# FFN of a hybrid attention/mLSTM step: weights requested a column block sooner, squares of gate and up summed by one product early in the block, group scale two units later

## The chip, the cores and the metric

The kernel runs on one core of a Trainium2 chip. The metric is device time in microseconds (us) of one execution; three executions were timed, and one more was taken with a profile. TensorE (PE, with its weight loads PEld), VectorE (DVE), ScalarE (ACT) and GpSimd (POOL) compute; SyncE (SP) issues most of the transfers.

## The reference, cut to what matters

One layer is computed for 128 context tokens and 1024 latent tokens (1152 rows, model width 1024): attention and a matrix-memory head group side by side, merged by an output projection, then a SwiGLU FFN of inner width 2816. The change touches the FFN alone:

```python
def swiglu(h, w_gu, w_down):
    g, u = jnp.split(h @ w_gu, 2, axis=-1)
    return (jax.nn.silu(g) * u) @ w_down
...
    h2 = rmsnorm(x, norm2_w) * (1 + sc2) + sh2
    x = x + g2 * swiglu(h2, w_gu, w_down)
```

`w_gu` is 1024 x 5632 (gate, then up), `w_down` 2816 x 1024, all in float32.

## The kernel before, in words

**Precision.** A float32 product is made of half-precision ones. Each weight or activation is multiplied by a power of two, rounded to float16 (`hi`), and the rest is kept as a second float16 (`lo`). A product is then hi x hi + hi x lo + lo x hi: three matmuls. The power of two comes from a measurement of the data.

**Pieces.** The inner width of 2816 is cut into 22 column blocks of 128, the class `Piece` (L1557 to L1621). A piece goes through these steps:
- `load` (L1562): two transfers of 512 KB, issued by SP (L1567), one for the gate's 128 columns and one for up's, into the ring `braw`, which has four buffers, so two pieces fit.
- `measure` (L1570): ACT squares each of the two and sums along the rows (L1577), into columns 0 and 1 of the small tile `v` (`fv`, five buffers).
- `scales` (L1579): a product with a matrix of ones (L1584) sums `v` over the partitions and gives every partition the result; eight short DVE instructions (L1587 to L1594) make the power of two and its inverses of it. In the kernel before there are four such products of one column each. Both output columns get the sum of gate and up, so both have the same scale.
- `convert` (L1596): `hi` by ACT (L1607) and `lo` by DVE (L1608), into `wpair` tiles; for gate and up themselves in the ring `whi`.
- `combine` (L1611): four DVE instructions (L1614 to L1617) turn the raw gate and up into sums and differences in place. `convert` with `sums=True` then splits these into the ring `wlo`, and after that the piece's `braw` buffers are free.
- `fold` (L1619): one DVE instruction that joins the inverse scales and that of `w_down`.

**Products.** The 1152 rows stand in three chunks of 384. For pieces 0 and 1 (`PLAIN`) each chunk gets 24 matmuls for gate and 24 for up (`products`, L1179: L1181 to L1183). From piece 2 on chunks 0 and 1 are computed together from seven half-length products (`half_products`, L1733: 12 matmuls each, L1736 to L1738), with DVE additions between them (L1778); chunk 2 follows with two full products. `activate` (L1740) makes silu(gate) x up with ACT (L1743), two DVE instructions (L1744, L1745) and measures the result with ACT (L1747).

**Units.** `gate_up9` (L1750) is a generator; what lies between two of its `yield`s is called a unit. A column block from piece 2 on has nine: the seven half products, n = 0 to 6, and the two full products, n = 7 and 8. At the end of each unit's products `hook(f, n)` (L1691) emits the preparation of the next pieces: in the kernel before, `load` of piece f + 2 at unit 0, `convert` of piece f + 1 at units 0 and 1, `combine` at 2, `convert` of the sums at 3 and 4, `measure` of piece f + 2 at 5 and 6, its `scales` at 7, and `fold` of f + 1 at 8. At units 0, 3 and 6 one step of `split_down` (L1533) prepares `w_down` and stores it in DRAM (L1554). For the first blocks `step` (L1672) holds a table of the same.

**Groups.** Pieces are taken in groups of 2, 4, 4, 4, 4 and 4 (`GROUPS`). When a group's activations are there, `rescale` (L1801) finds their common power of two: DVE finds the maximum over the rows (L1805), PE turns it into a row, DVE makes the power of two (L1808, `powers`, L163 to L166), and after a `yield` a product spreads it (L1812) and DVE copies it (L1813). Then ACT (L1817) and DVE (L1818) split each of the group's activation tiles into `hl`, twelve in a group of four. `down9` (L1842) multiplies these by the stored `w_down` (L1835 to L1837), loading it again in pieces of 512 KB (L1828) into buffers of the rings `raw` and, each third, `whi`; the result is added to the residual by DVE (L1136, L1137).

`groups9` (L1855) weaves this: three units of the next group's first column block, the first half of `rescale`, three units, the second half, three units, and then the down product. In the last group the down product is given out in parts between units.

**Order.** The FFN isn't ordered by hand. The program's order gives each instruction a priority, and a scheduler simulates the engines when the kernel is built: an engine that is free takes the ready instruction that stands first in the program. A transfer or an instruction can so be moved ahead of its place as soon as its buffer and its inputs are there. The order in which each engine executes is fixed by that simulation. Only the attention stage before it (until L1656) is ordered by hand; piece 0 is prepared there.

Of the kernel before, what the change touches and what calls it, by code (L numbers as in the profile page):

```python
# [12 lines left out]
I32 = mybir.dt.int32  # L13
AF = mybir.ActivationFunctionType
ALU = mybir.AluOpType
# [16 lines left out]
NF = D_FF // P  # L32
# [14 lines left out]
def hybrid_step(ctx: ExitStack, tc: tile.TileContext, I: dict, O: dict):  # L47
    nc = tc.nc
    mm = nc.tensor.matmul
    act = nc.scalar.activation  # L50
    dve = nc.vector
# [183 lines left out]
    wds = cp.tile([P, NF, 4], F32, name="wds")  # L235
    h2s = cp.tile([P, 2], F32, name="h2s")
# [3 lines left out]
    ones = cp.tile([P, P], F32, name="ones")  # L240
# [42 lines left out]
    ps = bank()  # L283
# [3 lines left out]
    ps = bank()  # L287
# [12 lines left out]
    for n in (1, 4):  # L300
        dve.tensor_scalar(out=bcol[:, n * KD : (n + 1) * KD], in0=bcol[:, n * KD : (n + 1) * KD],
                          scalar1=1.0, scalar2=None, op0=ALU.add)
# [110 lines left out]
    for c in range(NCH):  # L413
        if c > 0:
            normalise(c * CB, CB)
        for i in range(CB):
# [4 lines left out]
            for half, ps in enumerate(xT[b] if b < 1 else transposed(b)):  # L421
                full = p0.tile([P, 4, P], F32, name=nm("full"), tag="full", bufs=3)
                for j in range(4):
# [4 lines left out]
                    else:  # L428
                        dve.tensor_scalar(
                            out=full[:, j, :], in0=ps[:, j * P : (j + 1) * P],  # L430
                            scalar1=scale1[:, k, cnd : cnd + 1], scalar2=shift1[:, k, cnd : cnd + 1],
                            op0=ALU.mult, op1=ALU.add)
# [1124 lines left out]
    class Piece:  # L1557
# [21 lines left out]
        def scales(self):  # L1579
            v = self.v  # L1580
            ps = bank()
            for j in range(2):
                for i in range(2):
                    mm(ps[:, j : j + 1], ones, v[:, i : i + 1], start=(i == 0), stop=(i == 1))  # L1584
            e = v[:, 0:2]
            bits = e.bitcast(I32)
            dve.tensor_scalar(out=e, in0=ps[:, 0:2], scalar1=2.0 ** -40, scalar2=None, op0=ALU.max)  # L1587
            dve.tensor_scalar(out=bits, in0=bits, scalar1=0x7F800000, scalar2=None, op0=ALU.bitwise_and)
            dve.tensor_scalar(out=bits, in0=bits, scalar1=1, scalar2=None, op0=ALU.logical_shift_right)
            dve.tensor_scalar(out=bits, in0=bits, scalar1=1, scalar2=127 * 2 ** 22, op0=ALU.mult, op1=ALU.add)  # L1590
            dve.tensor_scalar(out=bits, in0=bits, scalar1=0x7F800000, scalar2=None, op0=ALU.bitwise_and)
            dve.tensor_scalar(out=v[:, 2:4].bitcast(I32), in0=bits, scalar1=-1, scalar2=267 * 2 ** 23, op0=ALU.mult, op1=ALU.add)
            dve.tensor_scalar(out=v[:, 4:6], in0=e, scalar1=2.0 ** -13, scalar2=h2s[:, 1:2], op0=ALU.mult, op1=ALU.mult)
            dve.tensor_scalar(out=v[:, 6:7], in0=v[:, 4:5], scalar1=0.5, scalar2=None, op0=ALU.mult)  # L1594

        def convert(self, js=(0, 1), sums=False):  # L1596
            if js[0] == 0:
                if sums:
                    self.t = []
                else:  # L1600
                    self.w = []
            for j in js:
                raw = self.raw[j]
                tag = "wlo" if sums else self.tags[j]
                t = wp.tile([P, 2, 1024], F16, name=nm("wpair"), tag=tag, bufs=5)
                sc = self.v[:, 2 + j : 3 + j]
                act(t[:, 0], raw, AF.Copy, scale=sc)  # L1607
                dve.scalar_tensor_tensor(out=t[:, 1], in0=raw, scalar=sc, in1=t[:, 0], op0=ALU.mult, op1=ALU.subtract)  # L1608
                (self.t if sums else self.w).append(tuple(t[:, i].rearrange("p (k n) -> p k n", k=KD) for i in range(2)))
# [8 lines left out]

        def fold(self):  # L1619
            v = self.v  # L1620
            dve.tensor_scalar(out=v[:, 7:8], in0=v[:, 4:5], scalar1=v[:, 5:6], scalar2=wds[:, self.f, 3:4], op0=ALU.mult, op1=ALU.mult)  # L1621


    pairs, late = {}, []
# [2 lines left out]
    with tc.manual_schedule(engines=ENGINES):  # L1627
# [21 lines left out]
        n = 0  # L1649
# [22 lines left out]
    def step(f, c, j):  # L1672

        at = (f, c, j)
        start = {
            (0, 0, 0): lambda: (pieces[0].fold(), pieces[1].measure(), next(wd_steps)),
            (0, 0, 1): lambda: (pieces[1].scales(), pieces[2].load(), next(wd_steps)),
            (0, 1, 0): lambda: (pieces[1].convert(), next(wd_steps)),
            (0, 1, 1): lambda: (pieces[2].measure(), next(wd_steps)),
            (1, 0, 0): lambda: (pieces[1].fold(), pieces[3].load(), next(wd_steps)),  # L1680
            (1, 0, 1): lambda: (pieces[2].scales(), next(wd_steps)),
            (1, 1, 0): lambda: (pieces[2].convert(), next(wd_steps)),
            (1, 1, 1): lambda: (pieces[2].combine(), next(wd_steps)),
            (0, 2, 0): lambda: (pieces[2].convert((0,), True),),
            (0, 2, 1): lambda: (pieces[2].convert((1,), True),),
            (1, 2, 0): lambda: (pieces[3].measure(),),
            (1, 2, 1): lambda: (pieces[3].scales(), pieces[2].fold()),
        }
        start[at]()

    def hook(f, n):  # L1691

        if n in (0, 3, 6):
            next(wd_steps, None)
        if n == 0 and f + 2 < NF:
            pieces[f + 2].load()
        if f + 1 < NF:
            p = pieces[f + 1]
            if n in (0, 1):
                p.convert((n,))  # L1700
            elif n == 2:
                p.combine()
            elif n in (3, 4):
                p.convert((n - 3,), True)
            elif n == 8:
                p.fold()
        if f + 2 < NF:
            if n in (5, 6):
                pieces[f + 2].measure((n - 5,))
            elif n == 7:  # L1710
                pieces[f + 2].scales()

    sums = [bp.tile([P, 2, 4, CT], F16, name=f"sum{i}") for i in range(2)]
# [141 lines left out]
    def groups9(grps):  # L1855

        held = None
        for g in grps:
            ups = gate_up9(g)
            if held is not None:  # L1860
                r = rescale(held)
                for _ in range(3):
                    yield next(ups)
                next(r)
                for _ in range(3):
                    yield next(ups)
                emit(r)
                for _ in range(3):
                    yield next(ups)
                d = down9(held)  # L1870
                if g is not grps[-1]:
                    yield from d
                    yield from ups
                else:
                    part = 3 * held["nf"]
                    for _ in range(part):
                        yield next(d)
                    for _ in range(18):
                        yield next(ups)
                    for _ in range(part):  # L1880
                        yield next(d)
                    yield from ups
                    for _ in range(part // 2):
                        yield next(d)
                    r = rescale(g)
                    next(r)
                    for _ in range(part // 4):
                        yield next(d)
                    emit(r)
                    yield from d  # L1890
            else:
                yield from ups
            held = g
# [91 lines left out]
```

## Time and profile before

| | us |
|---|---|
| three timed executions | 1636.68, 1638.21, 1641.33 |
| their median | 1638.21 |
| the profiled execution | 1635.57 |
| its span, first to last instruction | 1633.8 |
| mean granted clock of TensorE | 0.955 |
| PE busy, whole span | 1471.4 |
| DVE busy, whole span | 1140.2 |
| ACT busy, whole span | 788.1 |

How the views are read: in a timeline each row has the start (us from the span's start), the duration, the engine, the line of the kernel, the operation, the tile written and those read, shapes, and a count where neighbours are merged; the brackets at the end give the idle time of the engine before it and what ended that. The waits give, for an instruction and the one that released it, the total, the number of times and the longest. The groups give a line's instructions with their busy time, the mean in ns, and the idle time before them. The stretches give for a window the busy time of PE, PEld, DVE, ACT and POOL with counts, then the granted clock as a share of full speed, the share of the DMA engines and GB/s. Matmuls are pipelined, so a duration of one overlaps the next.

The FFN's dense part runs from about 840 us to 1573 us; what follows is the last group's down product with the final norm.

### The profile page before, as it was taken

The numbers are of one execution on the slowest core, as the hardware profiler recorded it, in microseconds if no ns is written. First come the engines' busy times: TensorE is split into PE (matmuls) and PEld (weight loads), VectorE is DVE, ScalarE is ACT, GpSimd is POOL, SyncE is SP. The second block draws the span as 40 slices with busy tenths as digits, with TensorE's granted clock in tenths as the row PEclk, the third lists the DMA queues.
The fourth block names the chain that finished last, engine by engine and source line by source line (L and its number), as shares of the span: only waits on it lengthen the run. The fifth ranks groups of instructions, "written<-read, shape, count | busy, mean of one in ns | idle before, by whom it ended". The sixth has DMA issues, their size and how long they took to land.

```text
span 1633.8 us, 23360 instructions
## 1 busy us (share of the span) xinstructions
PE 1471.4 (90%) x8549; PEld 914.1 (56%) x8549; DVE 1140.2 (70%) x2550; ACT 788.1 (48%) x1504; POOL 265.4 (16%) x284
## 2 busy tenths in 40 slices
PE   5899999898597799887789999999999999999995
PEld 1755666576354677665555466455545545556542
DVE  3844356849766877877579877767865766687478
ACT  3743343455465666778665345234414523454123
POOL 0411021313224522334341000000000000000001
PEclk8999999999698899998789999999999999999998
DMA  9345461301384789566444333423432342332303
GB/s 355 116 142 146 98 155 52 73 1 19 72 175 87 150 189 195 103 102 128 73 129 142 104 106 101 132 75 116 129 114 67 104 129 65 116 91 78 103 1 116
DMA packets 281688, 181.84 MB, mean 111 GB/s; under 512 B 167302, under 2 KB 253782, under 8 KB 281574
## 3 DMA queue, kind: packets, MB, share of 16 engines
q1 hardware_dynamic: 280150, 177.96, 42.0%
q10 hardware_dynamic: 1424, 2.40, 0.4%
q8 instruction: 67, 1.10, 0.3%
q14 instruction: 47, 0.39, 0.1%
HBM read 122.71 MB, written 19.29 MB: 87 GB/s over the span
## 4 chain that ended last, share of the span: by engine, by line
PE 32%; DVE 11%; ACT 4%; issue 3%; POOL 0%; DVEq 0%; ACTq 0%; POOLq 0%
PE mm L1835 5%; PE mm L1836 5%; PE mm L1837 4%; PE mm L1736 3%; PE mm L1738 3%; PE mm L1737 3%; PE mm L1181 3%; PE mm L1182 3%; PE mm L1183 3%; DVE wpair L1608 2%; ACT wpair L1607 1%; DVE sk L1725 1%; DVE tn L1778 1%; ACT jk L1577 1%; DVE x L1137 1%
## 5 line engine op out<-in xcount | busy, mean ns | idle before, releaser
L1607 ACT ACTIVATE wpair<-braw,fv 128x1024 f16<-128x1024 f32 x84 | 92.3, 1140 | 182.8 <-PE mm L1837 97.5
L1835 PE MATMUL mm<-wd,hl 128*128 128x512 f16 x396 | 150.2, 379 | 0.0
L1836 PE MATMUL mm<-wd,hl 128*128 128x512 f16 x396 | 150.0, 379 | 0.0
L1837 PE MATMUL mm<-wd,hl 128*128 128x512 f16 x396 | 148.2, 379 | 0.0
L1111 PE MATMUL S<-kst,qT 128*128 128x512 f32 (+1 forms) x384 | 98.2, 397 | 49.1 <-ACT pr L1119 47.4
L1181 PE MATMUL mm<-h,wpair 128*128 128x384 f16 x416 | 138.7, 333 | 2.8 <-DVE r L1190 2.8
L1182 PE MATMUL mm<-h,wpair 128*128 128x384 f16 x416 | 138.8, 334 | 0.0
L1183 PE MATMUL mm<-h,wpair 128*128 128x384 f16 x416 | 138.3, 333 | 0.0
L1926 POOL TENSOR_TENSOR x<-x,fw 128x512 f32<-128x512 f32 x9 | 11.7, 1303 | 741.2 <-ACT jk L1923 741.2
L500 PE MATMUL wi<-ipair,hT 128*128 128x384 f16 (+2 forms) x384 | 124.5, 325 | 2.8 <-ACT ipair L217 2.8
L501 PE MATMUL wi<-ipair,hT 128*128 128x384 f16 (+2 forms) x384 | 124.5, 324 | 0.0
L502 PE MATMUL wi<-ipair,hT 128*128 128x384 f16 (+2 forms) x384 | 124.0, 324 | 0.0
L1608 DVE SCALAR_TENSOR_TENSOR wpair<-braw,fv,wpair 128x1024 f16<-128x1024 f32 x84 | 106.9, 1279 | 23.6 <-ACT wpair L1607 23.3
L1518 DVE SCALAR_TENSOR_TENSOR pl<-pr,st,ph 128x1152 f16<-128x1152 f32 x64 | 97.6, 1525 | 30.4 <-ACT ph L1510 27.8
L1115 DVE TENSOR_REDUCE st<-S 128x1 f32<-128x1152 f32 x64 | 86.7, 1355 | 39.3 <-PE S L1111 38.7
L1510 ACT ACTIVATE ph<-pr,st 128x1152 f16<-128x1152 f32 x64 | 80.3, 1254 | 69.1 <-issue 60.8
L1111 PEld LDWEIGHTS S<-kst,qT 128*128 128x128 f32 x384 | 70.6, 210 | 73.6 <-ACT pr L1119 59.9
L1136 DVE SCALAR_TENSOR_TENSOR t<-mm,gm,gl 128x512 f32<-128x512 f32 x96 | 71.3, 744 | 29.1 <-PE mm L1837 28.8
L1119 ACT ACTIVATE pr<-S,st 128x1152 f32<-128x1152 f32 x64 | 78.0, 1219 | 24.5 <-DVE st L1115 23.7
L1747 ACT ACTIVATE jk<-tn 128x384 bf16<-128x384 f32 x66 | 34.3, 520 | 103.2 <-DVE tn L1745 97.1
L1137 DVE TENSOR_TENSOR x<-x,t 128x512 f32<-128x512 f32 x108 | 79.3, 736 | 1.4
L1737 PE MATMUL mm<-h,wpair 128*128 128x384 f16 x240 | 78.3, 326 | 0.0
(461 smaller groups left out, 3700.8 us busy)
## 6 DMA issues: line engine op xcount, KB each, us to landing
wd<-wd_d SPq DMA_DIRECT2D x58, 512.0 KB
braw<-in_w_gu_dram SPq DMA_DIRECT2D x44, 512.0 KB
a4s<-in_w_ada_dram SPq DMA_DIRECT2D x32, 512.0 KB
wdt<-in_w_down_dram SPq DMA_DIRECT2D x22, 512.0 KB
wd_d<-wdt SPq DMA_DIRECT2D x22, 512.0 KB
aw<-in_w_ada_dram SPq DMA_DIRECT2D x16, 512.0 KB
x<-in_x_sample_dram SPq DMA_DIRECT2D x16, 512.0 KB
iraw<-in_w_in_dram SPq DMA_DIRECT2D x32, 256.0 KB
```

Source lines behind the costliest of these rows:

```text
L500: mm(ps[:, :n], ah, wh[:, k % 2, c0 : c0 + n], start=(k == 0), stop=False)
L501: mm(ps[:, :n], ah, wl[:, k % 2, c0 : c0 + n], start=False, stop=False)
L502: mm(ps[:, :n], al, wh[:, k % 2, c0 : c0 + n], start=False, stop=(k == KD - 1))
L1111: mm(S[:, lo:hi], qTs[b][:, h, :], kst[kv][:, t, lo:hi], start=(t == 0), stop=(t == 1))
L1181: mm(ps, wh[:, k, :], th[:, k, :], start=(k == 0), stop=False)
L1182: mm(ps, wh[:, k, :], tl[:, k, :], start=False, stop=False)
L1183: mm(ps, wl[:, k, :], th[:, k, :], start=False, stop=(k == KD - 1))
L1608: dve.scalar_tensor_tensor(out=t[:, 1], in0=raw, scalar=sc, in1=t[:, 0], op0=ALU.mult, op1=ALU.subtract)
L1737: mm(ps, wh[:, k], al[:, k], start=False, stop=False)
L1835: mm(ps, ah, w[:, k, 0], start=(j + k == 0), stop=False)
L1836: mm(ps, ah, w[:, k, 1], start=False, stop=False)
L1837: mm(ps, al, w[:, k, 0], start=False, stop=(j + k == g["nf"] - 1))
```

## The change

`scales` makes one product, two columns wide, in place of four of one column: the sums of gate and up come out side by side. DVE copies the two, adds them with the floor of 2^-40 (one instruction more than before), and the following instructions work on one column in place of two; `convert` and `fold` read that one. In `hook` the load at unit 0 for piece f + 2 becomes a load at unit 5 for piece f + 3, the measuring goes from units 5 and 6 to units 1 and 2, and `scales` from unit 7 to unit 5. In `step` piece 4 is loaded with the measuring of piece 3. In `groups9` the second half of `rescale` comes after five units in place of three, and one unit in place of three follows it ahead of the down product.

```diff
         def scales(self):
             v = self.v
             ps = bank()
-            for j in range(2):
-                for i in range(2):
-                    mm(ps[:, j : j + 1], ones, v[:, i : i + 1], start=(i == 0), stop=(i == 1))
-            e = v[:, 0:2]
+            mm(ps[:, 0:2], ones, v[:, 0:2], start=True, stop=True)
+            e = v[:, 0:1]
             bits = e.bitcast(I32)
-            dve.tensor_scalar(out=e, in0=ps[:, 0:2], scalar1=2.0 ** -40, scalar2=None, op0=ALU.max)
+            dve.tensor_copy(v[:, 4:6], ps[:, 0:2])
+            dve.scalar_tensor_tensor(out=e, in0=v[:, 4:5], scalar=2.0 ** -40, in1=v[:, 5:6], op0=ALU.max, op1=ALU.add)
...
-            dve.tensor_scalar(out=v[:, 2:4].bitcast(I32), in0=bits, scalar1=-1, scalar2=267 * 2 ** 23, op0=ALU.mult, op1=ALU.add)
-            dve.tensor_scalar(out=v[:, 4:6], in0=e, scalar1=2.0 ** -13, scalar2=h2s[:, 1:2], op0=ALU.mult, op1=ALU.mult)
+            dve.tensor_scalar(out=v[:, 2:3].bitcast(I32), in0=bits, scalar1=-1, scalar2=267 * 2 ** 23, op0=ALU.mult, op1=ALU.add)
+            dve.tensor_scalar(out=v[:, 4:5], in0=e, scalar1=2.0 ** -13, scalar2=h2s[:, 1:2], op0=ALU.mult, op1=ALU.mult)
...
-                sc = self.v[:, 2 + j : 3 + j]
+                sc = self.v[:, 2:3]
...
-            (1, 2, 0): lambda: (pieces[3].measure(),),
+            (1, 2, 0): lambda: (pieces[3].measure(), pieces[4].load()),
...
-        if n == 0 and f + 2 < NF:
-            pieces[f + 2].load()
+        if n == 5 and f + 3 < NF:
+            pieces[f + 3].load()
...
         if f + 2 < NF:
-            if n in (5, 6):
-                pieces[f + 2].measure((n - 5,))
-            elif n == 7:
+            if n in (1, 2):
+                pieces[f + 2].measure((n - 1,))
+            elif n == 5:
                 pieces[f + 2].scales()
...
                 for _ in range(3):
                     yield next(ups)
                 next(r)
-                for _ in range(3):
+                for _ in range(5):
                     yield next(ups)
                 emit(r)
-                for _ in range(3):
-                    yield next(ups)
+                yield next(ups)
                 d = down9(held)
```

More of the change, by code (lines that the diff above doesn't have):

```diff
@@ L1620, in fold @@
             v = self.v
-            dve.tensor_scalar(out=v[:, 7:8], in0=v[:, 4:5], scalar1=v[:, 5:6], scalar2=wds[:, self.f, 3:4], op0=ALU.mult, op1=ALU.mult)
+            dve.tensor_scalar(out=v[:, 7:8], in0=v[:, 4:5], scalar1=v[:, 4:5], scalar2=wds[:, self.f, 3:4], op0=ALU.mult, op1=ALU.mult)
     pairs, late = {}, []
```

## The prediction

> **What bounds the kernel now.** I read the page first, then busy time by stage, then who waited for whom, and last the timelines of a few column blocks.
>
> ```profile
> span 1633.8 us, 23360 instructions
> ...
> PE   5899999898597799887789999999999999999995
> ...
> 840.00:1573.00 733.00, 715.43 (x4100) 403.76 (x4099) 528.90 (x1047) 298.47 (x529) 15.71 (x13) 0.99 0.32 101
> ```
>
> The last row is the FFN from the busy times by stage: length, then PE, PEld, DVE, ACT and POOL busy, granted clock, DMA share, GB/s. PE is busy 715.43 of 733.00 us, so it sets the end there, and 17.6 us are idle. DVE has 528.90 us and ACT 298.47: room on average. The waits name all of the idle time:
>
> ```profile
> PE mm L1584 <- ACT jk L1577: 13.8, 11, 2.0
> PE mm L1812 <- DVE gv L166: 3.8, 5, 1.0
> ...
> ACT wpair L1607 <- PE mm L1837: 97.5, 7, 20.9
> ```
>
> 13.8 + 3.8 = 17.6. The small product that sums the squares (L1584) waits 11 times for ACT's measuring (L1577), the group scale (L1812) 5 times for DVE. Since PE is dense otherwise, each of these microseconds, and each instruction taken off PE here, should shorten the run one to one, unless another engine then comes last. The third row, ACT waiting for a buffer, serves a rival below.
>
> **Part 1: three of four small products go.** Their count, and two places where they stand:
>
> ```profile
> L1584 PE MATMUL mm<-fv,ones 128*128 128x1 f32 x168 | 22.3, 239 | 13.8 <-ACT jk L1577 13.8
> ...
> 1000.11 0.33 PE L1183 MATMUL mm<-h,wpair 128*128 128x384 f16 x1
> 1000.28 0.28 PE L1584 MATMUL mm<-fv,ones 128*128 128x1 f32 x2
> 1000.42 0.32 PE L1181 MATMUL mm<-h,wpair 128*128 128x384 f16 x1
> ...
> 1005.94 0.33 PE L1737 MATMUL mm<-h,wpair 128*128 128x384 f16 x1
> 1006.10 0.72 PE L1584 MATMUL mm<-fv,ones 128*128 128x1 f32 x6
> 1006.69 0.32 PE L1738 MATMUL mm<-h,wpair 128*128 128x384 f16 x1
> ```
>
> The first row groups them from 830 us on. Each f32 product stands as two records, so a piece has 8, and 168 records are 21 pieces. I read costs from start to start, since matmuls overlap. A 384-wide product takes 0.16 (1000.11 to 1000.28). A pair takes 1000.42 - 1000.28 = 0.14 us, six take 1006.69 - 1006.10 = 0.59. The change keeps one product, two columns wide, which I price as a pair. Six records of 0.59 us go per piece: 21 x 0.59 = **12.4 us**. (Where eight stand together the saving is a little more; I leave that out.) DVE gets one short instruction more per piece, 9 in place of 8; this is taken up in part 4.
>
> **Part 2: squares measured at units 1 and 2, product behind unit 5.** A stall of now, first PE, then ACT:
>
> ```profile
> 1115.12 0.33 PE L1183 MATMUL mm<-h,wpair 128*128 128x384 f16 x1
> 1117.31 0.38 PE L1584 MATMUL mm<-fv,ones 128*128 128x1 f32 x2 [1.87 <-ACT jk L1577]
> ...
> 1110.26 2.19 ACT L1607 ACTIVATE wpair<-braw,fv 128x1024 f16<-128x1024 f32 x2 [6.40 <-DVE braw L1617]
> 1115.61 0.52 ACT L1747 ACTIVATE jk<-tn 128x384 bf16<-128x384 f32 x1 [2.65 <-DVE tn L1745]
> 1116.13 1.04 ACT L1577 ACTIVATE jk<-braw 128x1024 bf16<-128x1024 f32 x1
> ```
>
> The measuring at 1116.13 stands in ACT's queue behind the conversions of 1110.26, which waited 6.40 us for DVE's combining (L1617). ACT took its work in that order, so PE waits for DVE through ACT. The scheduler orders ready work by its place in the program. With the measuring at units 1 and 2 it comes ahead of those conversions (units 3 and 4) and falls into ACT's 6.40 idle us, which hold both squares (1.04 each and a short read-out). The product, behind unit 5, then finds its sums ready.
>
> Two of the 11 waits I keep, because their place does not really change. Piece 3 is measured in the plain blocks as before. Piece 4's load goes out at 904.33 (released by a split, as below), behind unit 5's products of block 2, so it can't be measured at units 1 and 2:
>
> ```profile
> 904.33 1.57 SPq L1567 DMA_DIRECT2D braw<-in_w_gu_dram  x2
> ...
> 888.62 0.83 PE L1584 MATMUL mm<-fv,ones 128*128 128x1 f32 x6 [0.66 <-ACT jk L1577]
> ...
> 910.35 0.38 PE L1584 MATMUL mm<-fv,ones 128*128 128x1 f32 x2 [1.97 <-ACT jk L1577]
> ```
>
> 13.8 - 0.66 - 1.97 = **11.2 us** go.
>
> What of the earlier load? Queue and release of the load in that same block:
>
> ```profile
> 1112.76 2.04 SPq L1567 DMA_DIRECT2D braw<-in_w_gu_dram  x2
> ...
> 1109.55 0.68 DVE L1617 TENSOR_TENSOR braw<-braw,braw 128x512 f32<-128x512 f32 x1
> 1111.44 1.28 DVE L1608 SCALAR_TENSOR_TENSOR wpair<-braw,fv,wpair 128x1024 f16<-128x1024 f32 x1 [0.75 <-ACT wpair L1607]
> 1113.11 1.28 DVE L1608 SCALAR_TENSOR_TENSOR wpair<-braw,fv,wpair 128x1024 f16<-128x1024 f32 x1
> ```
>
> The load goes out at 1112.76, as soon as the first split (1111.44 + 1.28 = 1112.72) gives its buffer back. That is ahead of the next block's unit 0, where the program asks for it: the scheduler has already hoisted it. Asking at unit 5 can't be sooner than the buffer. I give the moved load **0**; on SP it passes nothing that it doesn't stand behind now.
>
> **Part 3: the clock.** Windows of 3.4 us around three of the 1.87 us stalls:
>
> ```profile
> 1253.60:1257.00 3.40, 1.53 (x11) 0.83 (x9) 1.19 (x3) 2.08 (x5) 0.00 (x0) 0.99 0.80 227
> 1257.00:1260.40 3.40, 3.40 (x13) 1.63 (x11) 1.18 (x2) 2.06 (x6) 0.00 (x0) 0.50 0.21 61
> 1280.90:1284.30 3.40, 1.69 (x11) 1.12 (x12) 1.17 (x2) 2.16 (x5) 0.00 (x0) 1.00 0.64 175
> 1284.30:1287.70 3.40, 3.40 (x23) 2.06 (x21) 0.33 (x2) 2.12 (x5) 0.00 (x0) 1.00 0.00 0
> 1400.30:1403.70 3.40, 3.40 (x13) 1.71 (x14) 1.18 (x2) 2.06 (x6) 0.00 (x0) 0.50 0.26 78
> 1427.60:1431.00 3.40, 3.40 (x13) 1.60 (x12) 0.24 (x1) 2.12 (x5) 0.00 (x0) 0.50 0.00 1
> ```
>
> Behind three stalls the granted clock is 0.50 for one window (13 products in place of 23 or 24), behind another, at 1284.30, it stays 1.00. In the window ahead of the drop at 1257.00 PE was busy 1.53 of 3.40 us, clearly under half; ahead of the one that kept its clock 1.69, just about half. I take it that a stall which fills over half of one window halves the clock of the next. With the stalls these drops go: 3 x 1.7 = **5.1 us**.
> The Trainium skill, TensorE: Matmul & The Clock Gate, Part 1 and its section on HAM oscillation, says the clock falls to half after an idle window of about 3.4 us and asks for no gaps beyond that; by it 1.87 us is too short, and the drops have another cause and stay. The rows speak against it here, and I take the rows.
>
> **Part 4: the group scale two units later.** One such block, PE, DVE, ACT, PE, and two steps of a scale chain:
>
> ```profile
> 1016.54 0.33 PE L1738 MATMUL mm<-h,wpair 128*128 128x384 f16 x1
> 1017.45 0.35 PE L1812 MATMUL mm<-gv,one 1*128 1x2 f32 x2 [0.58 <-DVE gv L166]
> ...
> 1018.30 0.14 DVE L1813 COPY gm<-mm 128x2 f32<-128x2 f32 x1
> 1022.50 2.20 DVE L1818 SCALAR_TENSOR_TENSOR hl<-tn,gm,hl 128x384 f16<-128x384 f32 x4
> ...
> 1020.50 2.12 ACT L1817 ACTIVATE hl<-tn,gm 128x384 f16<-128x384 f32 x4
> ...
> 1028.36 0.38 PE L1835 MATMUL mm<-wd,hl 128*128 128x512 f16 x1
> 1028.57 0.38 PE L1836 MATMUL mm<-wd,hl 128*128 128x512 f16 x1
> ...
> 1099.08 0.17 DVE L1588 TENSOR_SCALAR fv<-fv 128x2 int32<-128x2 int32 x1
> 1099.28 0.17 DVE L1589 TENSOR_SCALAR fv<-fv 128x2 int32<-128x2 int32 x1
> ```
>
> The scale's product now stands behind unit 6 and the first full product, 36 x 0.16 = 5.8 us later, and DVE's chain, late by 0.6 to 1.0 us, is done by then. All five waits go: **3.8 us**.
>
> What is late next are the splits (L1817, L1818), which wait for the scale. Now they begin on DVE 4.2 us behind the scale, and the down product starts 1028.36 - 1018.30 = 10.1 us behind it. Afterwards only one full product lies between, 24 x 0.16 = 3.9 us, with 0.3 for the scale's own product. Its first block of rows needs splits 0 and 3, done after 0.85 (product to copied scale) + 0.5 + 2.2 = 3.6 of these 4.2 us if DVE is free; then 6 and 9, after 0.85 + 0.5 + 10 x 0.55 + 1.2 (an activation between, two instructions about as long as a split) = 8.1; they are needed 18 down products of 0.21 = 3.9 us later than the first, at 8.1. So it fits with no room. DVE must be free for it, and the scale chain of the next piece, 9 steps of 0.2 us from start to start, moves into the same block. I bound the new wait by 0 and 1.7 us in each of five groups, and take 0.6, near the lower end, since in program order DVE's backlog comes first and is shorter by then: **3 us lost**.
>
> **The sum.** 12.4 + 11.2 + 5.1 + 3.8 - 3 = 29.5 us. The profiled execution took 1635.57 us, its span 1633.8 of it; 1635.57 - 29.5 = 1606.1. The median of the timed runs is 1638.21, 2.6 higher, so I forecast 1638.2 - 29.5 = 1608.7, rounded **1609 us**.
>
> **The rivals.**
> (a) The clock drops aren't caused by the stalls and stay: 5.1 us less gain, 1638.2 - 24.4 = 1614. For it: the stall before 1284.30 had no drop. Against: all three drops begin at a stall. The page's rule above is this rival's reason. Chance 0.12.
> (b) The stall moves to the start of the down product: DVE's 4.2 us of backlog lies behind the later scale too. Counted from the copied scale, splits 0 to 3 are then ready after 4.2 + 2.2 = 6.4 us, and the down product starts after 4.2 - 0.85 = 3.3: 3.1 us x 5 = 15.5 in place of the 3 I took; with a halved window each (1.7 x 5 = 8.5) 24. Left: 32.5 - 15.5 = 17 down to 32.5 - 24 = 8.5, so 1621 to 1630. For it: DVE has no idle stamp in that stretch now. Against: that backlog is program-earlier work, which ends with PE's units. Chance 0.17.
> (c) Slower. The braw load, due at unit 5, heads SP's queue ahead of the down weights, while the conversions that release its buffer wait on a buffer that only a down product frees (the 97.5 us row). PE runs dry in the down stage until the chain has run: 1.14 + 1.28 + 4 x 0.68 + 1.14 + 1.28 = 7.6 us and 2.0 for issuing both loads, 9.6; four long down stages, and a halved window each: 4 x (9.6 + 1.7) = 45, against 32.5 won: 1651. It decides as soon as it costs over 8 us a stage. Against: loads stand in such stretches now without a PE wait. Chance 0.04.
> (d) Nothing measurable: the gaps reappear behind other waits of the same in-order queues, only the 12.4 us of the products are won, and the upper bound at the splits, 1.7 x 5 = 8.5, is lost: 1634. Chance 0.05 for within 0.3% (about 5 us, what a measurement here can tell from no change).
>
> **How the numbers follow.** The forecast has 0.62. Its own bounds: 0 for the splits' wait and both kept waits gone gives 32.5 + 2.6 = 35, with the eight-record places 36 to 38, so 1600; the upper bound of 1.7 x 5 gives 24, 1614. Range 1600 to 1622: it takes in (a) and the lighter half of (b); left out are the rest of (b), (c) and (d), under 0.2. Faster 0.62 + 0.12 + 0.17 = 0.91; same 0.05; slower 0.04.
>
> **What would show it.** Right: from 830 us on 42 records in L1584's group in place of 168, and no 1.87 us wait in it; the measuring ahead of the second conversions on ACT; no wait at L1812; clock 1.00 throughout 1240 to 1440; loads still released by the splits. Wrong: a PE wait at L1835 for L1818, PE waiting for a DMA in the down stage, or clock rows of 0.50 without a stall ahead.

## The result, and the profile after

The changed kernel takes **1611.12 us** (median of 4 runs, 1608.89 to 1613.40); the kernel before, run beside it, 1639.24 (4 runs, 1636.68 to 1641.33). The ratio is 0.9829, 95% interval 0.9809 to 0.9850: 28 us gained, where 29.5 were forecast. The profiled execution took 1611.04 us.

The page of the kernel after, its span and the busy tenths of PE:

```profile
span 1609.3 us, 23125 instructions
...
PE   5899999899596799987769999999999999999995
```

Busy times by stage of the kernel after (length, then PE, PEld, DVE, ACT, POOL busy, granted clock, DMA share, GB/s): the whole FFN, and the stretch of it in which the kernel before had its half-clock windows.

```profile
840.60:1542.60 702.00, 696.35 (x3962) 388.36 (x3961) 530.75 (x1074) 300.38 (x529) 16.36 (x13) 0.99 0.34 107
1239.00:1440.00 201.00, 200.81 (x1161) 113.25 (x1159) 154.24 (x321) 94.35 (x164) 0.00 (x0) 1.00 0.35 110
```

The FFN, from its first full product to the last group's scale product, is 702.0 us long; the same two points lie 731.8 apart in the kernel before (these lengths are good to 0.1 us). So **29.8 us** are won there, and PE's idle time falls from 17.6 to 5.6 us. It starts 4.6 us later in this profile (840.6 against 836.0). Of these, 4.5 us stand already at piece 0's small product (785.6 against 781.1), and up to there the instructions of both kernels are the same; the FFN's start varies from run to run (842.7 when the same kernel was profiled again). What PE still waits for in the FFN of the kernel after (us in all, times, longest; the waits that end with its first product or ahead of it are left out):

```profile
PE mm L1183 <- DVE wpair L1607: 2.4, 1, 2.4
PE mm L1582 <- ACT jk L1577: 1.7, 1, 1.7
...
PE mm L1181 <- ACT wpair L1606: 0.6, 1, 0.6
PE mm L1181 <- DVE sk L1724: 0.5, 1, 0.5
```

The small product (now L1582) waits once in place of eleven times. The group scale (now L1811) and the down product (now L1834) don't stand here at all. Two places are new: L1183 and L1181 are full products in the plain blocks at the FFN's start, and they wait for conversions. The small product's instructions, from 830 us on:

```profile
L1582 PE MATMUL mm<-fv,ones x42: 167/251/272, 850.5 to 1459.6; 128*128 128x2 f32 x42
```

42 records, two for each of 21 pieces, as forecast. Now one block of the steady part: ACT, then SP's queue, in the kernel after.

```profile
1101.15 2.19 ACT L1606 ACTIVATE wpair<-braw,fv 128x1024 f16<-128x1024 f32 x2 [3.87 <-DVE braw L1616]
...
1105.16 1.04 ACT L1577 ACTIVATE jk<-braw 128x1024 bf16<-128x1024 f32 x1
...
1106.19 1.04 ACT L1577 ACTIVATE jk<-braw 128x1024 bf16<-128x1024 f32 x1
```

```profile
1103.64 1.56 SPq L1567 DMA_DIRECT2D braw<-in_w_gu_dram  x2
```

Both squares are measured by 1107.3 and their product runs at 1111.00, with 3.7 us to spare. But the measuring still stands *behind* the second conversions (1101.15), not ahead of them as I had it, here and in every other block of the steady part. The wait went because the product now stands further behind the measuring. The load still goes out as soon as a split frees its buffer.

### The profile page after: what moved, and what is told of

It reads as the page before. It is cut to its first block, busy times and chain, and to the rows that moved or that the text cites. A ratio compares the mean times of both kernels' runs of the same rounds, so it can differ in the third digit from the quotient of the medians.

```text
span 1609.3 us, 23125 instructions
## 1 busy us (share of the span) xinstructions
PE 1456.1 (90%) x8417; PEld 900.6 (56%) x8417; DVE 1141.5 (71%) x2572; ACT 790.6 (49%) x1504; POOL 265.9 (17%) x284
## 5 line engine op out<-in xcount | busy, mean ns | idle before, releaser
L1835 PE MATMUL mm<-wd,hl 128*128 128x512 f16 x396 | 149.8, 379 | 0.0
L1834 PE MATMUL mm<-wd,hl 128*128 128x512 f16 x396 | 149.6, 379 | 0.0
L1836 PE MATMUL mm<-wd,hl 128*128 128x512 f16 x396 | 142.3, 379 | 0.0
L1181 PE MATMUL mm<-h,wpair 128*128 128x384 f16 x416 | 137.3, 330 | 4.3 <-DVE r L1190 3.2
L1183 PE MATMUL mm<-h,wpair 128*128 128x384 f16 x416 | 136.8, 330 | 2.4 <-DVE wpair L1607 2.4
L1182 PE MATMUL mm<-h,wpair 128*128 128x384 f16 x416 | 137.2, 330 | 0.0
L1518 DVE SCALAR_TENSOR_TENSOR pl<-pr,st,ph 128x1152 f16<-128x1152 f32 x64 | 94.3, 1474 | 28.2 <-ACT ph L1510 25.6
L1737 PE MATMUL mm<-h,wpair 128*128 128x384 f16 x240 | 78.2, 326 | 0.0
L1736 PE MATMUL mm<-h,wpair 128*128 128x384 f16 x240 | 78.2, 326 | 0.0
```

The source lines that it names most:

```text
L1181: mm(ps, wh[:, k, :], th[:, k, :], start=(k == 0), stop=False)
L1182: mm(ps, wh[:, k, :], tl[:, k, :], start=False, stop=False)
L1183: mm(ps, wl[:, k, :], th[:, k, :], start=False, stop=(k == KD - 1))
L1736: mm(ps, wh[:, k], al[:, k], start=False, stop=False)
L1737: mm(ps, wl[:, k], ah[:, k], start=False, stop=(k == 3))
L1834: mm(ps, ah, w[:, k, 0], start=(j + k == 0), stop=False)
```

## The experiments

Each kernel ran beside the kernel before on the same chip. The edits are against the changed kernel unless the text says "before".

**1. The product alone** (before, with the one-product scales and what follows from them; all places as before).

```
-            for j in range(2):
-                for i in range(2):
-                    mm(ps[:, j : j + 1], ones, v[:, i : i + 1], start=(i == 0), stop=(i == 1))
+            mm(ps[:, 0:2], ones, v[:, 0:2], start=True, stop=True)
...
             if n in (5, 6):
                 pieces[f + 2].measure((n - 5,))
             elif n == 7:
                 pieces[f + 2].scales()
```

> Only the one product in place of four; units and group scale as before. My theory (three separate sources): the 12.4 us of the six records go, and what else goes depends on where the single product is placed. If the waits came from measuring late (my prediction), the single product still waits for ACT at its place, about 13.8 us in all, the half-speed windows stay, and the time is 1639 - 12 = 1627. Rival 1: the waits came from the first of the four products, which needed one sum only and was sent early; one product needs both sums, is placed later and waits no more: 1639 - 12 - 11 - 5 = 1611, the whole change. Rival 2: the small products lie beside the others' time and cost nothing: 1639.

Measured: 1676.61 us, ratio 1.0240 (1.0222 to 1.0258). **38 us slower**, with 12 us of work less. Waits of PE in the FFN, then PE and ACT around one of them:

```profile
PE mm L1582 <- ACT jk L1577: 48.7, 18, 5.5
```

```profile
1043.55 0.33 PE L1183 MATMUL mm<-h,wpair 128*128 128x384 f16 x1
1047.71 0.37 PE L1582 MATMUL mm<-fv,ones 128*128 128x2 f32 x1 [3.83 <-ACT jk L1577]
```

```profile
1043.49 2.62 ACT L1816 ACTIVATE hl<-tn,gm 128x384 f16<-128x384 f32 x5
...
1046.52 1.04 ACT L1577 ACTIVATE jk<-braw 128x1024 bf16<-128x1024 f32 x1
```

The four old products could run in two steps: one pair needed only the gate's square, and in the trace of before it stood alone (the x2 of 1000.28), full products filling the time until the other three pairs ran (the x6 of 1006.10). The one product needs both squares at once, and up's is measured at unit 6. In four of the 18 blocks with a wait it stands behind splits of the group on ACT, as here (3.8 us each). In the other 14 it stands behind the measuring of an activation (L1746), which itself waits 1.3 us for DVE; one of these, where PE's small product waited 1.94 us until 1121.23:

```profile
1119.52 0.52 ACT L1746 ACTIVATE jk<-tn 128x384 bf16<-128x384 f32 x1 [1.34 <-DVE tn L1744]
...
1120.05 1.04 ACT L1577 ACTIVATE jk<-braw 128x1024 bf16<-128x1024 f32 x1
```

So PE waits up to 5.5 us a block, and the clock falls to half for 46.4 us of the FFN, where it was 14.8. My expectation and both rivals (1611 to 1639) missed: none had the wait grow. The terms of my sum don't stand by themselves: the product is only a saving once the measuring is early.

**2. Early measuring alone** (before, with four products, the load and the group scale in their old places).

```
-            if n in (5, 6):
-                pieces[f + 2].measure((n - 5,))
-            elif n == 7:
+            if n in (1, 2):
+                pieces[f + 2].measure((n - 1,))
+            elif n == 5:
                 pieces[f + 2].scales()
```

> Only the measuring at units 1 and 2 and the scale at unit 5; four products, the load at unit 0 and the group scale as before. Theory: waits of 11 to 12 us and three half-speed windows (5 us) go, the records stay: 1639 - 16.5 = 1622, with 168 records in the group. Rival 1 (the first of four products is sent early whatever the place of the measuring): the waits stay in part, 1630 to 1639. Rival 2 (all the gain is waits): 1611 to 1615.

Measured: 1619.41 us, ratio 0.9897 (0.9878 to 0.9915). Its waits:

```profile
PE mm L1584 <- ACT jk L1577: 0.8, 2, 0.4
PE mm L1812 <- DVE gv L166: 0.6, 1, 0.6
```

13.0 of the 13.8 us at L1584 go, and 3.2 of the 3.8 at the group scale, which wasn't touched; the three half-clock windows between 1257 and 1431 us go too (5.1). 13.0 + 3.2 + 5.1 = 21.3; the FFN is 21.3 us shorter (710.5). (The match is closer than the parts are: by the table further down waits and clock make 20.6, since in this trace a half-clock window from the stage ahead reaches further into the FFN.) The time is 2.6 us below the 1622 expected, which had left the group scale's waits standing. This single move is the change's main part.

**3. The group scale alone** (before, with the rescale split into 3, 5 and 1 units).

```
-                for _ in range(3):
+                for _ in range(5):
                     yield next(ups)
                 emit(r)
-                for _ in range(3):
-                    yield next(ups)
+                yield next(ups)
```

> Only the group scale two units later. Theory: the five waits for the scale go, 3.8 us, and the splits are done in time: 1635, no wait of the down product for its splits. Rival: the splits come late, 0 to 3 us in each of five groups: 1635 to 1650.

Measured: 1627.77 us, ratio 0.9942 (0.9926 to 0.9957). The FFN shortens by 9.6 us, to 722.2. The five waits of 3.8 us are gone, nothing waits at the down product, and the small products' waits fall as well:

```profile
PE mm L1584 <- ACT jk L1577: 11.0, 7, 2.0
```

Taken alone it is worth more than its own wait, and the time lies below both expectations (1635 and above): 2.8 us of the small products' waits went too, and half-clock time fell from 14.8 to 11.4 us. On top of the rest it is worth what the next run shows.

**4. The whole change but the group scale** (the rescale back at 3, 3 and 3 units).

> The whole change but the group scale, which stays after three units. Theory: the change's time plus the five waits, 1611 + 3.8 = 1615, with waits of 0.5 to 1.0 us at the scale's product in the trace. Rival: DVE has more room with the measuring early, the waits for the scale go by themselves, and the time is 1611.

Measured: 1611.14 us, ratio 0.9840 (0.9819 to 0.9861), not to be told from the whole change. My 1615 was wrong and the rival right: no wait at L1811 is left to remove here either. Its FFN is 705.1 in the trace, 3.1 us longer, and the difference sits in the clock (15.5 us of it at half, against 7.6); the timed runs don't show these 3.1 us.

**5. The whole change again.**

> The changed kernel once more, beside its variants on one chip: 1609 to 1613, about 28 us below the kernel before. What differs between its two traces ahead of 780 us is not of the change, since both kernels have the same instructions there.

Measured: 1611.42 us, ratio 0.9835 (0.9817 to 0.9853). FFN 702.0, as before to the tenth.

**6. The load left at unit 0.**

```
-        if n == 5 and f + 3 < NF:
-            pieces[f + 3].load()
+        if n == 0 and f + 2 < NF:
+            pieces[f + 2].load()
```

> The whole change but the load, which stays at unit 0 for the piece two blocks on. Theory: a load goes out when its buffer comes free, wherever the program asks for it: the time of the change within 2 us, and loads still released by the splits. Rival: the earlier request is what lets the measuring stand at units 1 and 2; without it the measuring waits for data, 5 to 15 us longer.

Measured: 1607.04 us, ratio 0.9819 (0.9803 to 0.9836), which overlaps the interval of run 5. FFN 702.0, with the same waits: the moved load is worth nothing there. The median is 4.4 us below run 5's, more than the 2 us that I had allowed; that lies outside the FFN, and its cause is not shown.

**7. The group scale one unit later still** (6 units, then 0).

```
-                for _ in range(5):
+                for _ in range(6):
                     yield next(ups)
                 emit(r)
-                yield next(ups)
```

> The change with the group scale one unit later still: behind the last full product, with nothing of the block left between it and the down product. Theory: the scheduler fills the time of the splits with units of the next block, which are ready, so the time stays within 2 us of the change. Rival (the stall at the splits, my rival b): at each of five groups the down product waits 0.85 + 0.5 + 2.2 = 3.6 us, 18 us in all, and half-speed windows behind it: 1629 to 1637.

Measured: 1622.81 us, ratio 0.9914 (0.9899 to 0.9929); FFN 714.5. The largest of its waits, then DVE just ahead of the copy of one group's scale (1172.96):

```profile
PE mm L1834 <- ACT hl L1816: 6.3, 5, 1.4
PE mm L1582 <- ACT jk L1577: 4.1, 1, 4.1
```

```profile
1172.49 0.56 DVE L1743 SCALAR_TENSOR_TENSOR tn<-t,mm 128x384 f32<-128x384 f32 x1 [4.99 <-PE mm L1183]
```

Here the down product does wait for the group's splits, in five groups, 6.3 us and not the 18 of the expectation. Rival (b) has the right place, but not the reason: DVE has no backlog here, it stood idle for 4.99 us. Both expected times missed.

**8. A buffer of its own for the measuring's unused output** (before, it shares the three buffers named t2 with other tiles; the measuring of w_down gets the same buffer, and its line is left out here).

```
-                jk = ft.tile([P, D], BF16, name=nm("jk"), tag="t2", bufs=3)
+                jk = junk(self.f)
...
+    def junk(f):
+        if f == 0:
+            return ft.tile([P, D], BF16, name=nm("jk"), tag="t2", bufs=3)
+        return bp.tile([P, D], BF16, name=nm("jk"), tag="mj", bufs=1)
```

> The change, and the throw-away output of the measuring (w_gu from piece 1 on and w_down) in a buffer of its own and no longer in the ring of three that the gated additions of DVE use. Theory: the one wait left at the small product, 1.7 us at 953, came from a measuring of w_down that stood 7.6 us behind such a buffer on ACT, with the piece's measuring behind it; it goes, and the time is 1 to 3 us less than the change. Rival: the measuring waits for something else there, and nothing changes.

Measured: 1630.86 us, ratio 0.9952 (0.9935 to 0.9968): 19 us slower than the whole change. The wait of 1.7 us at the small product is gone. Waits of PE, waits of ACT, and ACT at one of its own:

```profile
PE mm L1839 <- ACT hl L1821: 12.8, 5, 3.6
```

```profile
ACT jk L1582 <- DMA braw<-in_w_gu_dram: 95.4, 36, 4.8
```

```profile
1218.80 1.06 ACT L1582 ACTIVATE jk<-braw 128x1024 bf16<-128x1024 f32 x1 [4.53 <-DMA braw<-in_w_gu_dram]
```

In this kernel L1582 is the measuring and L1839 the down product. With a free buffer the measuring was put earlier in ACT's order, ahead of the landing of its weights, and ACT works in order: it stood 95.4 us for this DMA, a wait that the whole change doesn't have at all. The group's splits then come late (the 12.8 us above). That they are late through the measuring, that the shared ring had kept the measuring from being too early, and why the scheduler set it there (its own idea of the landing) is argued from the order, not shown. The 1 to 3 us that I expected to win didn't come.

**9. The clock by itself.** This kernel computes nothing of the layer: 63 dense stretches of 61 to 91 products of 128x384, and between them waits on an ACT operation of nine sizes.

```
for rep in range(7):
    for n in SIZES:
        count = 61 + 5 * rep
        ...
        for k in range(count):
            nc.tensor.matmul(p[:, 0:384], w[:, 0:128] if k == 0 else a[:, k % 4, 0:128], ...)
        act(sc[:, ...], p[:, 0:1], AF.Copy, scale=1e-4)
        act(w[:, 0:n], xf[:, 0:n], AF.Copy, scale=sc[:, ...])
        ...
```

> No part of the layer is computed (all outputs are zeros); it measures the clock alone: 63 stretches of 61 to 91 dense matmuls of 128x384, and between two of them a wait of PE for a chain of two ACT instructions of nine lengths, for waits of about 1 to 4 us, each at seven places against the clock's windows. My theory: the clock drops to half for the next window of 3.4 us when PE was idle for over half of a window, so waits under 1.7 us never drop it, waits between 1.7 and 3.4 us drop it only where they lie mostly in one window, and from 3.4 us on always. Rival (the page's rule): only waits that fill a window, 3.4 us or more, drop it, and the drops in the kernel before had another cause.

In this one profiled execution the clock changes only at the edges of a fixed grid of 3.413 us. Two windows of that grid with a stall, each with the window behind it:

```profile
198.55:201.96 3.41, 1.40 (x9) 0.65 (x8) 0.00 (x0) 1.88 (x2) 0.00 (x0) 1.00 0.00 0
201.96:205.37 3.41, 3.41 (x13) 1.67 (x11) 0.00 (x0) 0.00 (x0) 0.00 (x0) 0.50 0.00 0
737.85:741.26 3.41, 1.45 (x9) 0.68 (x7) 0.00 (x0) 1.88 (x2) 0.00 (x0) 1.00 0.00 0
741.26:744.67 3.41, 3.36 (x21) 2.07 (x22) 0.00 (x0) 0.00 (x0) 0.00 (x0) 1.00 0.00 0
```

2.01 us idle in the first window (3.41 - 1.40): half clock in the next. 1.96 in the third: full clock in the next. Over the run, every full-clock window of the 12 with 2.01 us idle or more was followed by a half one, and none of those with 1.96 or less; 13 of these had 1.75 to 1.96. The edge lies at 2.0 us, about 59% of a window. A wait counts only by what falls into one window: one of 2.76 us split as 1.95 and 0.8 kept the clock, and so did one of 3.42 split as 1.93 and 1.49 (at 789.05). So both expectations missed: waits of 1.75 to 1.96 us in a window didn't drop the clock, 3.42 didn't always, and 2.01 was enough. From half clock less will do: the half-clock window at 123.45, with 1.32 us idle, was followed by another one, those with 0.52 or less by full clock.

**10. Eight steps in place of nine in the first pieces** (the two sums added by accumulating products where f is below 4).

```
+            if self.f < 4:
+                for i in range(2):
+                    mm(ps[:, 0:1], ones, v[:, i : i + 1], start=(i == 0), stop=(i == 1))
+                dve.tensor_scalar(out=e, in0=ps[:, 0:1], scalar1=2.0 ** -40, scalar2=None, op0=ALU.max)
+            else:
                 mm(ps[:, 0:2], ones, v[:, 0:2], start=True, stop=True)
```

> The whole change, but in the pieces with f below 4 (those whose scales fall into the plain blocks and the first blocks after them) the two sums of squares are added by two accumulating small products into one column, which takes the copy out of the chain on VectorE (eight steps in place of nine). Theory: the changed kernel lost about 5 us in its plain blocks because the longer chain brings piece 1's conversions late; then the 2.43-us wait at L1183 behind VectorE's second half and the half-clock window at 865 should go, the stretch of the plain blocks shortens by 2 to 5 us, and the time is 1606 to 1609. Rival: the chain's length is not it (VectorE's additions of the half sums between its steps are, and they lie where they lay); then the wait stays over 1.5 us and the time is that of the whole change, 1611.

Measured: **1604.92 us**, ratio 0.9791 (0.9772 to 0.9810). First DVE in the plain blocks of the kernel after, then of this one: the first and the last step of piece 1's scale chain, and the conversions' second halves that need it; then PE in the kernel after, and the waits of this one.

```profile
851.67 0.15 DVE L1585 COPY fv<-mm 128x2 f32<-128x2 f32 x1
...
859.33 0.14 DVE L1593 TENSOR_SCALAR fv<-fv 128x1 f32<-128x1 f32 x1
...
863.11 2.47 DVE L1607 SCALAR_TENSOR_TENSOR wpair<-braw,fv,wpair 128x1024 f16<-128x1024 f32 x2
```

```profile
850.37 0.14 DVE L1587 TENSOR_SCALAR fv<-mm 128x1 f32<-128x1 f32 x1
...
855.76 0.14 DVE L1598 TENSOR_SCALAR fv<-fv 128x1 f32<-128x1 f32 x1
...
857.88 1.27 DVE L1612 SCALAR_TENSOR_TENSOR wpair<-braw,fv,wpair 128x1024 f16<-128x1024 f32 x1
```

```profile
861.69 0.32 PE L1182 MATMUL mm<-h,wpair 128*128 128x384 f16 x1
864.44 0.34 PE L1183 MATMUL mm<-h,wpair 128*128 128x384 f16 x1 [2.43 <-DVE wpair L1607]
```

```profile
PE mm L1589 <- ACT jk L1577: 1.5, 1, 1.5
PE mm L1586 <- ACT jk L1577: 0.7, 1, 0.7
```

Lengths are compared here, not times, since the FFNs start at 840.6 and 838.7. The chain takes 7.7 us from first to last step in the kernel after, 5.4 here and in the kernel before, which has eight steps too. Between most steps DVE does an addition for the inputs of the half products (L1724 in the kernel after, 0.55 to 1.16 us each), so one step more opens one more such gap, about 1.2 us with the step. The rest of the 2.3 us comes of how the additions fall between the other steps. The wait of 2.43 us is gone, with the half-clock window behind it, and the FFN is 698.3 us, 3.7 shorter; nearly all of it lies in the plain blocks (55.9 to 52.5 us from the first full product to the first half product). The other traces agree: in each one with nine steps (runs 1, 4 to 8, 11 and the kernel after) PE waits 2.7 to 3.6 us in all for conversions and half sums there, and in those with eight (before, runs 2, 3, 10, 12) 0.3 us at most. The time is 6.5 us below run 5's; the part beyond the FFN's 3.7 lies outside it and is not explained.

**11. The product alone, with its scales at unit 8** (run 1, one unit later).

```
-            elif n == 7:
+            elif n == 8:
                 pieces[f + 2].scales()
```

> The one product alone with the measuring left in units 5 and 6 of the block, as in the first experiment, but with the scales moved from unit 7 to unit 8. Theory: what cost 48.7 us of TensorE's waits there was only that the one product stands too close behind its second measuring, so a unit more of distance (about 14 us) takes the waits down to under 6 us and the time to 1610 to 1622. Rival: the chain behind the product is then too late for the conversions in units 0 and 1 of the next block, and the waits turn up at the full products behind ScalarE's or VectorE's conversions; then it stays at 1630 or above.

Measured: 1638.27 us, ratio 0.9996 (0.9979 to 1.0013). Its waits, and ACT ahead of one of them (PE's small product of that block waited 2.65 us, until 1033.30):

```profile
PE mm L1582 <- ACT jk L1577: 18.4, 9, 2.7
PE mm L1811 <- DVE gv L166: 5.5, 5, 1.1
```

```profile
1029.08 2.62 ACT L1816 ACTIVATE hl<-tn,gm 128x384 f16<-128x384 f32 x5
...
1032.12 1.04 ACT L1577 ACTIVATE jk<-braw 128x1024 bf16<-128x1024 f32 x1
```

Both expectations were wrong in part. A unit of distance takes 30 of the 48.7 us away, so distance is most of it. But nine waits stay, at the same place and not at the conversions. In four of them up's square still stands behind ACT's splits, as here (2.65 us each); in the other five (1.5 to 1.6 us each) it stands behind the measuring of an activation that waits 1.3 us for DVE. It has to be measured earlier, too.

**12. Run 10 with the load at unit 0.**

> The whole change with the sums by two accumulating products for f below 4, and the load left at unit 0. If the two small savings are real and add up, it is 1602 to 1606; if the load at unit 0 is worth nothing, it equals the run with the sums alone within 2 us.

Measured: 1604.58 us, ratio 0.9788 (0.9769 to 0.9807); FFN 698.3. The same as run 10. The load's place is worth nothing, for the second time; run 10 and this one beat both kernels.

## Why the prediction was right

The mechanism was right in the main: PE's small products, its waits and the clock are what the change takes away, 29.5 us by the forecast and 29.8 in the traces. That the total comes within 0.3 us is luck, since errors of 1 to 4 us in its terms cancel. Take from the FFN's length PE's waits and half of the time at half clock:

| kernel | FFN us | PE waits | at half clock | what is left |
|---|---|---|---|---|
| before | 731.8 | 17.6 | 14.8 | 706.8 |
| 2, early measuring | 710.5 | 1.7 | 5.4 | 706.1 |
| 3, group scale | 722.2 | 11.0 | 11.4 | 705.5 |
| 1, product | 770.5 | 53.2 | 46.4 | 694.1 |
| 11, product, unit 8 | 731.7 | 27.2 | 22.6 | 693.2 |
| 8, own buffer | 719.9 | 20.2 | 14.3 | 692.6 |
| 7, six units | 714.5 | 14.6 | 15.6 | 692.1 |
| 4, no group scale | 705.1 | 5.9 | 15.5 | 691.5 |
| after | 702.0 | 5.6 | 7.6 | 692.6 |
| 10, eight steps | 698.3 | 2.6 | 5.2 | 693.1 |

What is left is 706 with four products and 693 with one, within 1.5 us over ten kernels whose FFN differ by 72. So PE's work, its waits and the clock account for the FFN to within 1.5 us.

**Part 1, products, 12.4.** 42 records remain, and the account gives 14.2 (706.8 to 692.6), the little more that I had left out included. Read from start to start over all places, the small products take 16.9 us before and 3.1 after, 13.8 less. A pair of two columns costs what one of one column did. What the step lacked is its condition: by itself the product costs 38 us (run 1), since it waits for the later of two squares.

**Part 2, waits on measuring, 11.2.** 12.1 went (13.8 to 1.7). The reason was half wrong. The measuring is not ahead of the second conversions; the product is further behind it. The two waits that I kept, at pieces 3 and 4, are gone, and the one left is piece 5's at 955.56. PE, then ACT, at that place in the kernel after:

```profile
955.56 0.38 PE L1582 MATMUL mm<-fv,ones 128*128 128x2 f32 x2 [1.71 <-ACT jk L1577]
```

```profile
952.25 1.06 ACT L1547 ACTIVATE jk<-wdt 128x1024 bf16<-128x1024 f32 x1 [7.64 <-DVE x L1137]
...
953.32 1.06 ACT L1577 ACTIVATE jk<-braw 128x1024 bf16<-128x1024 f32 x1
```

The measuring stands behind that of w_down (L1547), which waited 7.64 us for a tile of the shared ring to come free. Run 8 gives the measuring another buffer: this wait goes, and more is lost elsewhere.

**The load, 0.** Right: runs 6 and 12.

**Part 3, the clock, 5.1.** The three windows went, and with them 5.1 us. But one new window came in the plain blocks of the kernel after:

```profile
865.30:868.70 3.40, 3.40 (x12) 1.62 (x11) 3.40 (x10) 1.08 (x3) 0.00 (x0) 0.50 0.95 267
```

It stands behind the wait of 2.43 us, as a stall should. The FFN's time at half clock went from 14.8 to 7.6 us: 3.6 won. My rule of half a window is too low: the edge is 2.0 of 3.413 us in run 9. The old stalls show 1.87 us idle in one window, which by that would just keep the clock. But they end in a small product, and run 1 has two windows that differ in that, each with the window behind it:

```profile
968.78:972.19 3.41, 1.47 (x10) 0.69 (x7) 1.18 (x2) 2.07 (x6) 0.00 (x0) 1.00 0.13 52
972.19:975.60 3.41, 2.72 (x18) 1.75 (x19) 1.36 (x9) 2.08 (x4) 0.00 (x0) 1.00 0.02 5
1265.69:1269.10 3.41, 1.48 (x10) 0.77 (x9) 1.18 (x2) 2.07 (x6) 0.00 (x0) 1.00 0.00 0
1269.10:1272.51 3.41, 3.41 (x13) 1.72 (x14) 1.99 (x10) 2.05 (x3) 0.00 (x0) 0.51 0.00 0
```

Both have 1.93 to 1.94 us idle. In the first the stall runs on into the next window, and the clock stays; in the second its small product (1268.92) stands inside, and the clock falls. If the gate doesn't count that product, the second has 2.1 us idle. The old three come to 2.0 to 2.1 in the same way (0.25 us from a small product to the next full one), and the stall ahead of 1284.30, which kept its clock, to 2.0, at the edge itself. In the plain blocks of runs 1, 4, 7 and 11 a window with only 1.55 to 1.67 us idle lost the clock too; without the small products and transposes in it, it comes to 1.95 to 2.01, again about the edge. So the traces speak for it; no run tried it by itself. The Trainium skill's page TensorE: Matmul & The Clock Gate, Part 1, gives a free-running window of 3413 ns, which these traces bear out; its fall after one idle window of about 3.4 us they do not, since 2.01 us were enough. Rival (a), built on that rule, is out.

**Part 4, the group scale, 3.8 less 3.** The waits went: 3.8. The 3 us at the splits did not come. DVE, then PE, at one group in the kernel after:

```profile
1161.03 0.16 DVE L1812 COPY gm<-mm 128x2 f32<-128x2 f32 x1 [1.32 <-PE mm L1811]
1161.90 5.38 DVE L1817 SCALAR_TENSOR_TENSOR hl<-tn,gm,hl 128x384 f16<-128x384 f32 x10 [0.71 <-ACT hl L1816]
```

```profile
1160.62 0.38 PE L1811 MATMUL mm<-gv,one 1*128 1x2 f32 x2
...
1164.84 0.38 PE L1834 MATMUL mm<-wd,hl 128*128 128x512 f16 x1
```

The splits begin on DVE 0.87 us behind the scale, not 4.2: its backlog is done by then, and DVE even waits for PE and ACT. The down product starts 3.8 us behind the scale without a wait. So rival (b) found no backlog to be late by. And the 3.8 weren't this part's alone: with the rest in place nothing waits there even at the old place (run 4).

**The sum.** Products 14.2, waits 12.0 (17.6 to 5.6), clock 3.6: 29.8, against 12.4, 11.2 + 3.8 - 3 = 12.0, and 5.1. The waits come out the same because two misses cancel: no loss of 3 at the splits and 0.9 more at the measuring, but 3.9 us of waits that I didn't forecast, nearly all in the plain blocks. The step that missed there is in part 1: I counted the ninth step of DVE's chain and took it up only at the splits, where there is room, and not in the plain blocks, where each step waits its turn behind the additions. Rivals (c) and (d) are out: no PE wait for a DMA stands in the FFN, and the gaps didn't come back elsewhere.

## What to carry to other kernels

Several small instructions can begin on the first of two inputs; before joining them into one that needs both, move the later input's producer well ahead, or the saving turns into a wait (12 us of work less, 38 us lost). An instruction added to a chain on a shared in-order engine costs the work that stands between two of its steps as well as its own time, so price it in the stage where that engine is full. And a producer can be too early as well: an in-order engine that reaches it ahead of its data holds everything queued behind it.

## What the runs showed of the hardware

The clock gate judges windows of a fixed grid of 3.413 us, and 2.0 us idle within one are enough for half clock in the next (12 of 12 windows from 2.01 up, none up to 1.96). So between such products stalls of up to 1.96 us, or longer ones of which no more than that falls into one window, cost only themselves, and longer ones cost 1.7 us more or not, by their place on the grid. Run 9 shows this for dense 16-bit products alone; that a small 32-bit product at the end of a stall isn't counted as work is what the old stalls of 1.87 us and the two windows of run 1 speak for, and wasn't tried by itself. A stall of 1.87 us that ends in one did cost a window.
